# A decoder layer on one core: gate and up projections as a 2x2 block product with seven products, the down projection as its own stage

## The chip, the cores and the metric

The kernel runs on one core of one Trainium2 chip. The metric is device time in microseconds of one execution, the median of several runs; less is better. TensorE (PE in the profile; PEld is its weight loads) multiplies, VectorE (DVE) and ScalarE (ACT) do element-wise work, GpSimd (POOL) issues some stores, and SyncE (SP) issues the loads, in program order.

## The reference

One hybrid decoder layer for 512 tokens of width 2048, in float32. Two attentions side by side, a memory cross-attention and a SwiGLU feed-forward follow each other, each with a scaled residual and a layer norm. The change concerns the last part (D_MODEL is 2048, D_FF is 5632):

```python
c = memory_cross_attention(h, mem, w_q_mem[l], w_kv_mem[l], w_o_mem[l])
h = layer_norm(ALPHA * h + c, ln2_g[l], ln2_b[l])
gate, up = jnp.split(h @ w_gate_up[l], 2, axis=-1)      # [512, 2048] @ [2048, 11264]
f = (jax.nn.silu(gate) * up) @ w_down[l]                # [512, 5632] @ [5632, 2048]
h = layer_norm(ALPHA * h + f, ln3_g[l], ln3_b[l])
```

## The kernel before

**Number format.** Products run in float32r. Every operand is split into hi (rounded to float32r) and lo = x - hi. `split` (L102 to 104) is one ScalarE cast that writes hi and one VectorE subtraction that writes lo. A product is three matmuls (`mm3`, L124 to 129): hi by hi, hi by lo, lo by hi.

**Weights.** A weight unit is 128 x 1024 numbers, 512 KB. SP loads it into a staging tile (`ws`, L112), then it is split. There are three buffers each of staging, hi and lo. `next_unit` keeps two units ahead of the one in use. The tile `wgu` is a unit of gate or up weights, `wdn` one of down weights.

**Order.** TensorE's and SP's instructions run in the order of the program text. VectorE's and ScalarE's are ordered by a scheduler as the kernel is built. `Side` places side work (layer norms, transposes) between the weight units.

**The feed-forward.** There are 44 hidden tiles f of 128 features. Gate and up of one f are each 2 units, 16 contraction blocks of 128, so 48 matmuls of 512 tokens each into one PSUM bank (`gate_up`, tile `gu`). `glu` makes silu(gate) times up and splits it into `fh` and `fl`, which stay in SBUF. The hidden tiles go in pairs, in chunks of 6, 6, 5, 3 and 2 pairs; behind the pairs of a chunk its down products run (`down`, tiles `dn_*`), 4 column blocks of 512, added into the residual `y`. So gate/up and down alternate.

**The first four hidden tiles.** While the second 256 tokens still go through layer norm 2, `swiglu_halves` runs the first 2 pairs for tokens 0 to 255 alone (tile `gh`, 256 columns), and then, with the same weights loaded again, for tokens 256 to 511. That is 768 matmuls of 256 columns; the other 40 hidden tiles are 3840 of 512 columns. `put` transposes the normed rows (`h2tr`) and splits them into `h2h` and `h2l`, the moving operands.

**The tail.** The down weights of the last 2 pairs are kept in SBUF (`resident`), so that the last products run by token block and layer norm 3 can begin early.

Of the kernel before, what the change touches and what calls it, by code (L numbers as in the profile page):

```python
# [1018 lines left out]
```

## Time and profile before

| | |
|---|---|
| runs | 2735.85, 2737.0, 2740.66 us; median 2737.0 us |
| span of the profiled execution | 2737.2 us |
| TensorE busy | 2709.0 us (99%) |
| VectorE, ScalarE busy | 1303.8 us (48%), 942.6 us (34%) |
| moved by DMA | 325.57 MB, 119 GB/s over the span |

The result gives no time of its own for the profiled execution beside its span; 0.2 us lie between the span and the median of the runs. A matmul's duration in the profile contains the filling and draining of the array, which overlap with its neighbours; how fast matmuls follow each other is read from their start times.

### The profile page before, as it was taken

Reading aid. Unit: us, or ns where it says so; the run is one execution under the profiler, and the core shown is the slowest. Engines: PE = TensorE matmul, PEld = TensorE weight load, DVE = VectorE, ACT = ScalarE, POOL = GpSimd, SP = SyncE. Lnnn points to the kernel's source line nnn. Section 1 sums busy time; section 2 is a strip of 40 time slices with the busy share of each in tenths; the row PEclk is TensorE's granted clock in tenths of the full one; section 3 lists DMA queues with packets and bytes.
Section 4 is the critical chain, followed back from the end, with each engine's and each line's share of the span. In section 5 each row is a group of like instructions: output and inputs, shape, how many; then the busy total and the mean of one; then the engine's idle time right before and its main releaser. Section 6 shows DMA issues by size and latency. Waiting matters only on the chain.

```text
span 2737.2 us, 33827 instructions
## 1 busy us (share of the span) xinstructions
PE 2709.0 (99%) x14024; PEld 2301.8 (84%) x14024; DVE 1303.8 (48%) x1659; ACT 942.6 (34%) x1338; POOL 67.7 (2%) x109
## 2 busy tenths in 40 slices
PE   9999999999999999999999999999999999999998
PEld 7877777899988889988988888888888888888886
DVE  4258888986523753459632223222232223323247
ACT  3246556664421453345522212222222222222230
POOL 0001110100000000000000000000000000000001
PEclk9999999999999999999999999999999999999999
DMA  5322222346732662345543233322323232332341
GB/s 180 103 79 69 74 74 77 109 154 198 249 123 97 234 239 93 108 149 175 182 142 99 94 100 93 100 95 98 99 94 100 94 100 96 96 100 93 100 138 62
DMA packets 91146, 325.57 MB, mean 119 GB/s; under 512 B 10480, under 2 KB 10736, under 8 KB 90992
## 3 DMA queue, kind: packets, MB, share of 16 engines
q1 hardware_dynamic: 87408, 310.83, 34.9%
q0 software_dynamic: 3584, 12.58, 1.2%
q8 instruction: 110, 1.80, 0.3%
q14 instruction: 44, 0.36, 0.0%
HBM read 306.59 MB, written 16.78 MB: 118 GB/s over the span
## 4 chain that ended last, share of the span: by engine, by line
PE 95%; DVE 2%; ACT 2%; issue 0%; POOL 0%; DMA 0%; DVEq 0%; SPq 0%; POOLq 0%
PE gu L127 11%; PE gu L129 11%; PE gu L128 11%; PE mvp L127 1%; PE pjkb L127 1%; PE mvp L129 1%; PE mkp L129 1%; PE mkp L128 1%; PE mkp L127 1%; PE gh L127 1%; PE gh L128 1%; PE kq L129 1%; PE gh L129 1%; PE kq L128 1%; PE mvp L128 1%; PE kq L127 1%
## 5 line engine op out<-in xcount | busy, mean ns | idle before, releaser
L104 DVE TENSOR_TENSOR wgu_1l<-wgu_1s,wgu_1h 128x1024 fp32r<-128x1024 f32 x96 | 117.6, 1225 | 324.6 <-ACT wgu_1h L103 324.6
L127 PE MATMUL gu<-h2h,wgu_0h 128*128 128x512 f32 x640 | 249.0, 389 | 0.0
L128 PE MATMUL gu<-h2l,wgu_0h 128*128 128x512 f32 x640 | 249.0, 389 | 0.0
L129 PE MATMUL gu<-h2h,wgu_0l 128*128 128x512 f32 x640 | 249.0, 389 | 0.0
L127 PE MATMUL gu<-h2h,wgu_1h 128*128 128x512 f32 x640 | 249.0, 389 | 0.0
L128 PE MATMUL gu<-h2l,wgu_1h 128*128 128x512 f32 x640 | 249.0, 389 | 0.0
L129 PE MATMUL gu<-h2h,wgu_1l 128*128 128x512 f32 x640 | 249.0, 389 | 0.0
L103 ACT CAST wgu_0h<-wgu_0s 128x1024 fp32r<-128x1024 f32 x96 | 101.0, 1053 | 370.7 <-PE gu L128 315.8
L103 ACT CAST wgu_1h<-wgu_1s 128x1024 fp32r<-128x1024 f32 x96 | 101.1, 1053 | 325.8 <-PE gu L128 152.9
L104 DVE TENSOR_TENSOR wgu_0l<-wgu_0s,wgu_0h 128x1024 fp32r<-128x1024 f32 x96 | 117.5, 1224 | 184.7 <-ACT wgu_0h L103 184.7
L129 PEld LDWEIGHTS gu<-h2h,wgu_0l 128*128 128x128 f32 x640 | 120.3, 188 | 25.0
L127 PEld LDWEIGHTS gu<-h2h,wgu_1h 128*128 128x128 f32 x640 | 120.3, 188 | 25.0
L128 PEld LDWEIGHTS gu<-h2l,wgu_0h 128*128 128x128 f32 x640 | 120.1, 188 | 25.1
L128 PEld LDWEIGHTS gu<-h2l,wgu_1h 128*128 128x128 f32 x640 | 120.2, 188 | 24.8
L129 PEld LDWEIGHTS gu<-h2h,wgu_1l 128*128 128x128 f32 x640 | 120.0, 188 | 24.9
L127 PEld LDWEIGHTS gu<-h2h,wgu_0h 128*128 128x128 f32 x640 | 120.0, 188 | 24.7
L848 DVE TENSOR_TENSOR sg<-sg,gu 128x512 f32<-128x512 f32 x40 | 27.5, 687 | 134.2 <-PE gu L129 134.2
L104 DVE TENSOR_TENSOR wdn_0l<-wdn_0s,wdn_0h 128x1024 fp32r<-128x1024 f32 x20 | 24.5, 1225 | 66.9 <-ACT wdn_0h L103 66.9
L104 DVE TENSOR_TENSOR wdn_2l<-wdn_2s,wdn_2h 128x1024 fp32r<-128x1024 f32 x20 | 24.5, 1225 | 66.1 <-ACT wdn_2h L103 66.1
L104 DVE TENSOR_TENSOR wdn_1l<-wdn_1s,wdn_1h 128x1024 fp32r<-128x1024 f32 x20 | 24.5, 1223 | 65.2 <-ACT wdn_1h L103 65.2
L104 DVE TENSOR_TENSOR wdn_3l<-wdn_3s,wdn_3h 128x1024 fp32r<-128x1024 f32 x20 | 24.5, 1224 | 63.3 <-ACT wdn_3h L103 63.3
L332 DVE TENSOR_TENSOR_SCAN a<-ones,nl 128x128 f32<-128x128 f32 (+3 forms) x64 | 49.8, 811 | 10.1 <-POOL nl L329 9.9
(1923 smaller groups left out, 7052.3 us busy)
## 6 DMA issues: line engine op xcount, KB each, us to landing
wgu_0s<-in_w_gu SPq DMA_DIRECT2D x96, 512.0 KB, 3.5
wgu_1s<-in_w_gu SPq DMA_DIRECT2D x96, 512.0 KB, 3.4
wdn_0s<-in_w_dn SPq DMA_DIRECT2D x22, 512.0 KB, 3.5
wdn_1s<-in_w_dn SPq DMA_DIRECT2D x22, 512.0 KB, 3.4
wdn_2s<-in_w_dn SPq DMA_DIRECT2D x22, 512.0 KB, 3.5
wdn_3s<-in_w_dn SPq DMA_DIRECT2D x22, 512.0 KB, 3.4
wmv_0s<-in_w_mv SPq DMA_DIRECT2D x16, 512.0 KB, 3.6
wmv_1s<-in_w_mv SPq DMA_DIRECT2D x16, 512.0 KB, 3.6
```

Of the source, the lines that this page charges most:

```text
L103: nc.scalar.copy(hi, src)
L104: return nc.vector.tensor_tensor(lo, src, f32(hi), op=ALU.subtract)
L127: nc.tensor.matmul(acc, lh, rh, start=first, stop=False)
L128: nc.tensor.matmul(acc, lh, rl, start=False, stop=False)
L129: nc.tensor.matmul(acc, ll, rh, start=False, stop=last)
L332: nc.vector.tensor_tensor_scan(a[:, h, :nk][:, ::-1], ones.to_broadcast([P, nk]), nlt[:, h, :nk][:, ::-1], 0.0, op0=ALU.mult, op1=ALU.add)
L848: nc.vector.tensor_tensor(sg, sg, ua, op=ALU.mult)
```

## The change

**The block product.** The 512 tokens by 2048 inputs are taken as 2x2 blocks: a11 (tokens 0 to 255, inputs 0 to 1023), a12, a21, a22. For each hidden tile the weights are 2x2 blocks too: input half by gate or up, 1024 x 128 each. The product of these, eight block products before, is made of seven, with sums on both sides:

- on the token side once: s1 = a21 - a22, s3 = a11 - a21, s2 = s1 - a11 and s4 = a12 + s2, each split into hi and lo, beside a11, a12 and a22;
- on the weight side for every hidden tile, by VectorE: three additions on a loaded piece `xw` (1024, 512 and 512 columns for four loaded blocks of 512), then the splits `wh` and `wl` of seven blocks, 1792 columns for each quarter of the contraction;
- on the result: the seven products lie in four PSUM banks (tile `zz`, two buffers), and `finish` adds them up in the tile `e`.

All matmuls of this stage have 256 moving columns. The weights come as pieces of 1 MB (`w_st`), two for each hidden tile, each into its own buffer (`x0`, `x1` of the pool `pq`, one each; `xw0` and `xw1` below). Three buffers of `wh` and `wl` hold the quarters.

**The early part.** In place of `swiglu_halves`, a11 and a12 times the gate weights of 12 hidden tiles (`EARLY`, tile `ge`, 576 matmuls of 256 columns) run while the second half of the tokens is normed. Their two results go to memory (`early_d`) and come back for `finish`; for these 12 tiles five products are left and five blocks (1280 columns) to split. The side work now also makes the sums and splits on the token side (`second_half`).

**Memory.** silu(gate) times up goes to memory (`f_d`, 1 MB for a pair), and so does `y` (`y_d`). The pools of SBUF and PSUM are closed and opened anew for the gate/up stage and once more for the down stage. That stage has chunks of 8, 6, 6 and 2 pairs and loads `fx`, `fh`, `fl` and `yf` through SP, between the weights. Its matmuls and its tail are as before.

The core of the diff:

```diff
-FF_CHUNKS = [6, 6, 5, 3, 2]
+FF_CHUNKS = [8, 6, 6, 2]
+EARLY = 12
...
+    for f in range(EARLY):
+        acc = ps_lin(f"ge{f}")
         for u in range(2):
             w = next_unit()
             for c in range(8):
-                mm3(a, at(w, ALL, cs(c, P)), at(hc(8 * u + c), ALL, cols), u == 0 and c == 0, u == 1 and c == 7)
+                mm3(acc[:, cs(u, 256)], at(w, ALL, cs(c, P)), a_block(("a11", "a12")[u], c), c == 0, c == 7)
             side.run(SIDE3)
+        e = otile(f"ee{f}")
+        urgent(nc.scalar.copy, e[:, 256:512], acc[:, 0:256])
+        urgent(nc.vector.tensor_tensor, e[:, 0:256], e[:, 256:512], acc[:, 256:512], op=ALU.add)
+        nc.gpsimd.dma_start(early_d[f], e)
+    side.drain()
+    (pq, ps) = open_pools(1, [("pq", 1), ("ps", 1)])
+    PRODUCTS = [("a11", 1, 2, 0), ("a12", 2, 0, 0), ("s4", 3, 1, 1), ("s1", 4, 3, 0), ("s3", 5, 2, 1),
+                ("s2", 6, 0, 1), ("a22", 7, 1, 0)]
...
+        for f, h in pieces:
+            x = pq.tile([P, 8, 512], F32, tag=f"x{h}", name=f"xw{h}")
+            lowest = 3 if f < EARLY else 1
+            nc.sync.dma_start(x[:, 0:4], io["w_st"][f, h].rearrange("p (b n) -> p b n", b=4))
+            nc.vector.tensor_tensor(x[:, 4:6], x[:, 1:4:2], x[:, 0:1].to_broadcast([P, 2, 512]), op=ALU.add)
+            nc.vector.tensor_tensor(x[:, 6], x[:, 4], x[:, 3], op=ALU.add)
+            nc.vector.tensor_tensor(x[:, 7], x[:, 6], x[:, 2], op=ALU.add)
+            for k in range(2):
+                hi = pq.tile([P, 7, 256], F32R, tag=f"wh{n % 3}", name=f"wh{n % 3}")
+                lo = pq.tile([P, 7, 256], F32R, tag=f"wl{n % 3}", name=f"wl{n % 3}")
+                src = x[:, lowest:8, cs(k, 256)]
+                split(hi[:, lowest - 1:7], lo[:, lowest - 1:7], src)
...
+    def finish(f, z, e):
+        e1 = e[:, 7]
+        tt = nc.vector.tensor_tensor
+        if f < EARLY:
+            urgent(tt, e[:, 2], e1, z[:, 0, 256:512], op=ALU.add)
+        else:
+            urgent(nc.scalar.copy, e1, z[:, 2, 0:256])
+            urgent(tt, e[:, 0:3:2], z[:, 0].rearrange("p (b n) -> p b n", b=2),
+                   e[:, 7:8].to_broadcast([P, 2, 256]), op=ALU.add)
+        urgent(tt, e[:, 1], e[:, 2], z[:, 2, 256:512], op=ALU.add)
+        urgent(tt, e[:, 5:7], z[:, 3:4, 0:256].to_broadcast([P, 2, 256]), e[:, 1:3], op=ALU.subtract)
+        urgent(tt, e[:, 3:5], e[:, 1:7:5], z[:, 1].rearrange("p (b n) -> p b n", b=2), op=ALU.add)
+        sg, fh, fl = otile(f"sg{f}"), otile(f"fh{f}", F32R), otile(f"fl{f}", F32R)
+        s2 = sg.rearrange("p (b n) -> p b n", b=2)
+        nc.scalar.activation(s2, e[:, 0:4:3], AF.Silu)
+        tt(s2, s2, e[:, 4:6], op=ALU.mult)
+        split(fh, fl, sg)
+        nc.gpsimd.dma_start(f_d[f // 2, 0][:, cs(f % 2, 512)], f32(fh))
+        nc.gpsimd.dma_start(f_d[f // 2, 1][:, cs(f % 2, 512)], f32(fl))
+    for f in range(NFT):
+        z = ps.tile([P, 4, 512], F32, tag="zz", name=f"zz{f}", bufs=2)
+        for step in range(4):
+            hi, lo = next_weights()
...
+                    for i, (l, r) in enumerate(((wh, ah), (wh, al), (wl, ah))):
+                        nc.tensor.matmul(out_, l, r, start=begin and i == 0 and bank not in seen,
+                                         stop=step == 3 and k == 1 and i == 2, skip_group_check=True)
...
+        finish(f, z, e)
+    pt, pw, pg, ps = open_pools(2, [("pt", 2), ("pw", 3), ("pg", 4), ("ps", 1)])
...
+                if first and nb == 0:
+                    if i + 2 < len(prs):
+                        fs[prs[i + 2]] = f_in_x(prs[i + 2])
+                    if i % 2 == 0:
+                        nc.sync.dma_start(y[i // 2][0], y_d[i // 2, 0])
+                if first and nb == 1 and i < len(chunks[1]):
+                    fs[chunks[1][i]] = f_in_m(chunks[1][i])
```

**VectorE inside the gate/up stage.** Before, in the middle of the stage: one hidden tile has four unit splits, one product `sg` and one split `fl`.

```order
L104 TENSOR_TENSOR wgu20_1_1l_15340<-wgu20_1_1s_15337,wgu20_1_1h_15339 128x1024
L104 TENSOR_TENSOR wgu21_0_0l_15371<-wgu21_0_0s_15368,wgu21_0_0h_15370 128x1024
L104 TENSOR_TENSOR wgu21_0_1l_15401<-wgu21_0_1s_15398,wgu21_0_1h_15400 128x1024
L848 TENSOR_TENSOR sg10_0_15428<-sg10_0_15428,gu20_1_15367 128x512
L104 TENSOR_TENSOR wgu21_1_0l_15437<-wgu21_1_0s_15434,wgu21_1_0h_15436 128x1024
L104 TENSOR_TENSOR fl10_15305<-sg10_0_15428,fh10_15304 128x512
```

Now, behind the twelfth hidden tile, part of the cycle of one hidden tile (`wl0` to `wl2` are the three weight buffers, `xw0` and `xw1` the two pieces):

```order
L983 TENSOR_TENSOR sg16_15304<-sg16_15304,e_15210 128x512
L116 TENSOR_TENSOR wl0_15417<-xw0_15411,wh0_15416 128x1792
L116 TENSOR_TENSOR fl16_15306<-sg16_15304,fh16_15305 128x512
L946 TENSOR_TENSOR xw1_15524<-xw1_15524 128x1024
L947 TENSOR_TENSOR xw1_15524<-xw1_15524 128x512
L948 TENSOR_TENSOR xw1_15524<-xw1_15524 128x512
L116 TENSOR_TENSOR wl1_15464<-xw0_15411,wh1_15463 128x1792
L116 TENSOR_TENSOR wl2_15530<-xw1_15524,wh2_15529 128x1792
L120 TENSOR_TENSOR e_15420<-zz17_15313,e_15420 128x2x256
L946 TENSOR_TENSOR xw0_15621<-xw0_15621 128x1024
L120 TENSOR_TENSOR e_15420<-e_15420,zz17_15313 128x256
L947 TENSOR_TENSOR xw0_15621<-xw0_15621 128x512
```

`wl1_15464` is the last reader of piece `xw0_15411`; the next piece in that buffer, `xw0_15621`, is loaded behind it and stands two VectorE instructions further on.

**VectorE where the 256-column products of the first half end.** Before:

```order
L104 TENSOR_TENSOR wgu1_3_0_1l_12341<-wgu1_3_0_1s_12338,wgu1_3_0_1h_12340 128x1024
L848 TENSOR_TENSOR sg1_0_1_12368<-sg1_0_1_12368,gh2_1_1_12307 128x256
L104 TENSOR_TENSOR wgu1_3_1_0l_12377<-wgu1_3_1_0s_12374,wgu1_3_1_0h_12376 128x1024
L104 TENSOR_TENSOR fl1_11391<-sg1_0_1_12368,fh1_11390 128x256
L104 TENSOR_TENSOR wgu1_3_1_1l_12407<-wgu1_3_1_1s_12404,wgu1_3_1_1h_12406 128x1024
```

Now, from the last early unit on (`hr01`, `s2`, `s4` belong to the token side):

```order
L116 TENSOR_TENSOR wge11_1l_12197<-wge11_1s_12194,wge11_1h_12196 128x1024
L854 TENSOR_TENSOR hr01_11294<-hr01_11294,hr00_11209 128x1024 x2
L116 TENSOR_TENSOR s2l_12257<-hr00_11209,s2h0_12255 128x1024
L116 TENSOR_TENSOR s2l_12257<-hr00_11209,s2h1_12256 128x1024
L120 TENSOR_TENSOR ee11_12292<-ee11_12292,ge11_12230 128x256
L116 TENSOR_TENSOR s4l_12287<-hr01_11294,s4h_12286 128x1024 x2
L946 TENSOR_TENSOR xw0_12307<-xw0_12307 128x1024
L947 TENSOR_TENSOR xw0_12307<-xw0_12307 128x512
L948 TENSOR_TENSOR xw0_12307<-xw0_12307 128x512
L946 TENSOR_TENSOR xw1_12320<-xw1_12320 128x1024
L116 TENSOR_TENSOR wl0_12313<-xw0_12307,wh0_12312 128x1280
```

Between the split of the last early unit and the first `wl` stand eleven VectorE instructions, where before the next unit's split followed.

**SP where the gate/up stage ends.** Before, at the first change from gate/up to down weights:

```order
L112 DMA wgu11_1_0s_13406<-in_w_gu 128x1024
L112 DMA wgu11_1_1s_13436<-in_w_gu 128x1024
L112 DMA wdn0_0s_13467<-in_w_dn 128x1024
L112 DMA wdn1_0s_13497<-in_w_dn 128x1024
L112 DMA wdn2_0s_13534<-in_w_dn 128x1024
```

Now:

```order
L945 DMA xw1_20774<-in_w_st 128x2048
L1021 DMA fx0_20992<-f_d_10634 128x1024 x2
L1021 DMA fx1_20995<-f_d_10634 128x1024 x2
L124 DMA wdn0_0s_21000<-in_w_dn 128x1024
L124 DMA wdn1_0s_21006<-in_w_dn 128x1024
L124 DMA wdn2_0s_21012<-in_w_dn 128x1024
L1021 DMA fx2_21018<-f_d_10634 128x1024 x2
L1044 DMA yf0_0_20984<-y_d_10632 128x1024
L124 DMA wdn3_0s_21046<-in_w_dn 128x1024
L1021 DMA fx3_21052<-f_d_10634 128x1024 x2
```

The first down weights now stand behind 2 MB of hidden tiles, and further megabytes stand between the weights that follow.

## Rows read from the trace of the kernel before

**Rows 1.** Page: span; busy us (share) and instructions of TensorE, VectorE, ScalarE.

```profile
span 2737.2 us, 33827 instructions
...
PE 2709.0 (99%) x14024; PEld 2301.8 (84%) x14024; DVE 1303.8 (48%) x1659; ACT 942.6 (34%) x1338; POOL 67.7 (2%) x109
```

**Rows 2.** Page: the chain of work that ended last, shares by engine.

```profile
PE 95%; DVE 2%; ACT 2%; issue 0%; POOL 0%; DMA 0%; DVEq 0%; SPq 0%; POOLq 0%
```

**Rows 3.** Waits of PE: engine, line, releaser: us in total, times, longest.

```profile
PE trb L351 <- ACT a L335: 9.4, 5, 1.9
PE zb L136 <- DVE qb L108: 0.3, 1, 0.3
```

**Rows 4.** By tile: matmuls, duration in ns min/median/max, first and last start us.

```profile
L127 PE MATMUL gu<-h2h,wgu_0h x640: 389/389/396, 1375.5 to 2609.7; 128*128 128x512 f32 x160
...
L127 PE MATMUL dn_0a<-wdn_0h,fh x80: 389/389/389, 1549.6 to 2630.8; 128*128 128x512 f32 x80
...
L127 PE MATMUL mkp<-mh,wmk_0h x128: 283/283/283, 645.7 to 734.6; 128*128 128x256 f32 x128
...
L129 PE MATMUL mkp<-mh,wmk_1l x128: 283/283/283, 648.8 to 737.8; 128*128 128x256 f32 x128
```

**Rows 5.** Busy us (instructions) by stretch: PE, PEld, DVE, ACT, POOL; clock, DMA share, GB/s.

```profile
1279.00:1327.00 48.00, 48.00 (x402) 47.84 (x401) 41.02 (x63) 31.90 (x42) 0.00 (x0) 1.00 0.57 176
1327.00:1375.50 48.50, 48.50 (x407) 48.50 (x406) 23.85 (x25) 19.75 (x25) 0.00 (x0) 1.00 0.66 207
1375.50:1549.60 174.10, 174.10 (x770) 144.19 (x770) 49.07 (x48) 41.76 (x49) 0.00 (x0) 1.00 0.32 106
```

**Rows 6.** Groups of VectorE by form: busy us, mean ns of one | idle before, releaser.

```profile
L104 DVE TENSOR_TENSOR wgu_1l<-wgu_1s,wgu_1h 128x1024 fp32r<-128x1024 f32 x96 | 117.6, 1225 | 324.6 <-ACT wgu_1h L103 324.6
...
L104 DVE TENSOR_TENSOR fl<-sg,fh 128x512 fp32r<-128x512 f32 x40 | 27.4, 684 | 0.0
...
L104 DVE TENSOR_TENSOR fl<-sg,fh 128x256 fp32r<-128x256 f32 x8 | 3.3, 416 | 0.5 <-ACT fh L103 0.5
```

**Rows 7.** Timeline of VectorE: start us, us, instruction [idle before].

```profile
1309.59 1.22 DVE L104 TENSOR_TENSOR wgu_1l<-wgu_1s,wgu_1h 128x1024 fp32r<-128x1024 f32 x1
1310.72 0.75 DVE L667 SCALAR_TENSOR_TENSOR y<-y,n2mv,ln_b 128x512 f32<-128x512 f32 x1
1311.38 1.22 DVE L104 TENSOR_TENSOR wgu_0l<-wgu_0s,wgu_0h 128x1024 fp32r<-128x1024 f32 x1
1312.52 1.28 DVE L104 TENSOR_TENSOR h2l<-h2tr,h2h 128x512 fp32r<-128x512 f32 x2
```

**Rows 8.** Groups of ScalarE by form.

```profile
L103 ACT CAST wgu_1h<-wgu_1s 128x1024 fp32r<-128x1024 f32 x96 | 101.1, 1053 | 325.8 <-PE gu L128 152.9 <-issue 148.6 <-PE dn_3d L129 13.2
...
L103 ACT CAST fh<-sg 128x512 fp32r<-128x512 f32 x40 | 24.5, 613 | 0.0
...
L847 ACT ACTIVATE sg<-gu 128x512 f32<-128x512 f32 x40 | 23.5, 588 | 0.0
```

**Rows 9.** DMA issues: queue, count, KB each, median us to landing.

```profile
wgu_0s<-in_w_gu SPq DMA_DIRECT2D x96, 512.0 KB, 3.5
...
wmk_1s<-in_w_mk SPq DMA_DIRECT2D x16, 512.0 KB, 4.3
...
out<-y SPq DMA_DIRECT2D x16, 256.0 KB, 2.4
```

**Rows 10.** DMA view of 640 to 740 us: GB/s in 40 slices of 2.5 us.

```profile
GB/s 111 193 203 7 198 246 244 328 144 216 357 246 239 203 208 43 279 313 216 259 238 203 267 238 61 224 326 172 221 292 239 221 228 180 128 262 244 221 236 262
```

**Rows 11.** Chain over 0 to 15 us, TensorE's first matmuls: start, us, what.

```profile
8.34 0.43 PE v0b L128
...
13.28 0.23 PE v0b L129
```

**Rows 12.** Timeline, down projection: a split ends, its buffer's next load is issued.

```profile
2002.36 1.23 DVE L104 TENSOR_TENSOR wdn_2l<-wdn_2s,wdn_2h 128x1024 fp32r<-128x1024 f32 x1 [4.22 <-ACT wdn_2h L103]
...
2003.62 0.33 SPq L112 DMA_DIRECT2D wdn_2s<-in_w_dn  x1
```

More of the change, by code (lines that the diff above doesn't have):

```diff
@@ L40 @@
 AHEAD = 2
-HALVED = 2
 TURN = 2
@@ L811, in layer, with put @@
     gb2 = load_gb("ln2_g", "ln2_b")
-    put, hc = transposed("h2")
+    y_d = dram.tile([NT, 2, P, 1024], F32, name="y_d")
+    early_d = dram.tile([EARLY, P, 512], F32, name="early_d")
+    f_d = dram.tile([NFT // 2, 2, P, 1024], F32, name="f_d")
+    raw = {}
+    blocks = {}
+    def put(t, nb, bank):
+        key = (t // 2, nb // 2)
+        if key not in raw:
+            raw[key] = xtile(1, [P, 8, 256], f"hr{key[0]}{key[1]}", F32)
+        tr = bank(f"h2tr{t}_{nb}")
+        for c in range(4):
+            o = (nb % 2) * 512 + c * P
+            nc.tensor.transpose(tr[:, cs(c, P)], y[t][nb // 2][:, o:o + P], ident)
+        c0 = (nb % 2) * 4
+        urgent(nc.scalar.copy, raw[key][:, c0:c0 + 4, cs(t % 2, P)], tr.rearrange("p (c n) -> p c n", c=4))
+        yield
@@ new lines, in block, with x_halves, of, m_halves @@
+    def block(name, tile_of):
+        hi, lo = tile_of(name + "h"), tile_of(name + "l")
+        blocks[name] = hi, lo
+        return hi, lo
+    def x_halves(half):
+        def of(name):
+            w = xtile(half, [P, 8, 256], name)
+            return [w[:, 0:4], w[:, 4:8]]
+        return of
+    def m_halves(name):
+        return [mtile([P, 4, 256], f"{name}{j}") for j in range(2)]
+    def split_block(name, src, hi, lo):
+        for j in range(2):
+            split(hi[j], lo[j], src[:, cs(j, 4)])
+            yield
@@ L813, in layer, with a_block, keep @@
+    def a_block(name, c):
+        hi, lo = blocks[name]
+        return hi[c // 4][:, c % 4], lo[c // 4][:, c % 4]
+    def keep(t):
+        for i in range(2):
+            nc.gpsimd.dma_start(y_d[t, i], y[t][i])
+        yield
     for half in range(2):
@@ new lines, in layer, with weights @@
+    pieces = [(f, h) for f in range(NFT) for h in range(2)]
+    ready = []
+    def weights():
+        n = 0
+        for f, h in pieces:
[10 more added lines that the diff above has]
+                split(hi[:, lowest - 1:7], lo[:, lowest - 1:7], src)
+                n += 1
+                yield hi, lo
@@ new lines, in layer, with y_tile, f_load, f_in_x @@
+    pt, pw, pg, ps = open_pools(2, [("pt", 2), ("pw", 3), ("pg", 4), ("ps", 1)])
+    def y_tile(t, i):
+        return mtile([P, 1024], f"yf{t}_{i}", F32) if t == 1 else ttile(t, [P, 1024], f"yf{t}_{i}")
+    y[:] = [[y_tile(t, i) for i in range(2)] for t in range(NT)]
+    def f_load(pr, tiles):
+        for part, ft in enumerate(tiles):
+            nc.sync.dma_start(f32(ft), f_d[pr, part].rearrange("p (c n) -> p c n", c=2))
+        return tiles
+    def f_in_x(pr):
+        ft = xtile(pr % 2, [P, 2, 2, 512], f"fx{pr}")
+        return f_load(pr, [ft[:, part] for part in range(2)])
@@ L889, in down, with f_in_m @@
+    def f_in_m(pr):
+        return f_load(pr, [mtile([P, 2, 512], f"fh{pr}"), mtile([P, 2, 512], f"fl{pr}")])
+    fs, res = {}, {}
+    def down(prs, blocks, first=False, ahead_of=None):
         for nb in blocks:
@@ L924, in resident @@
                     yield
-    down(chunks[-2], f1, [0])
+    source = down_units()
+    c0, c1, c2, c3 = chunks
+    for pr in c0[:2]:
+        fs[pr] = f_in_x(pr)
+    down(c0, range(4), first=True)
+    gb = load_gb("ln3_g", "ln3_b")
+    down(c1, range(4), ahead_of=c2)
+    fs[c2[-1]] = f_in_m(c2[-1])
+    tc.keep_in_program_order(nc.scalar.preload_act_table_set("natural_log_exp_and_others"))
+    down(c2, [0])
     side.add(resident())
-    down(chunks[-2], f1, [1, 2, 3])
+    down(c2, [1, 2, 3], ahead_of=c3)
     side.drain()
```

166 lines of the change are left out of this document (85 added, 81 removed).

## The prediction

> **What bounds the kernel now.** I read the page first: TensorE is busy for 99% of the span [rows 1], and the chain of work that ended last is 95% TensorE [rows 2]. The view of waits confirms it: the longest sum of TensorE's waits on one releaser is 9.4 us, all in the attention [rows 3]. In the feed-forward it never waits. VectorE is busy for less than half of the span, but in the stretch that the early part takes the place of it is busy for 41.0 of 48 us [rows 5], so the mean hides where it is short. What the change can win is therefore how fast matmuls follow each other; what it can lose is the cover that the other engines and the loads now give TensorE without a gap.
>
> **Matmul rates.** Durations overlap, so I take starts. The 8 hidden tiles from 1375.5 us to the first down product at 1549.6 us are 768 matmuls of 512 columns: 0.2267 us each. The `mkp` stage is 768 matmuls of 256 columns from 645.7 to 737.8 us: 0.1201 us each [rows 4]. Two short ones cost 6% more than a long one.
>
> **Products.** Before, gate/up is 3840 x 0.2267 + 768 x 0.1201 = 870.5 + 92.2 = 962.7 us. Now it is 12 x 48 early, 12 x 120 and 32 x 168, together 7392 matmuls of 256 columns: 887.8 us. The change takes away 74.9 us, not an eighth of 962.7 (120), since all columns now run at the dearer rate. The down products (2112 matmuls of 512) are equal.
>
> **Prices on VectorE and ScalarE.** A VectorE operation of 1024, 512, 256 columns takes 1225, 684, 416 ns [rows 6], but the next independent one starts about 0.085 us before its end (1309.59 to 1310.72 us) [rows 7]: 1.14, 0.60, 0.33 us in a row. No row has 1280 or 1792 columns; on the same line they are 1.41 and 1.95 us. ScalarE's cast takes 1053 and 613 ns for 1024 and 512 [rows 8], so 1.27 and 1.71 us. A waiting engine starts some 0.03 us behind its releaser [rows 12].
>
> **A 1 MB load.** The trace has none, and much hangs on it; call its time to landing L. 512 KB land in 3.5 us, 256 KB (stores) in 2.4 us [rows 9]. On that slope L is 3.5 + 2 x 1.1 = 5.7 us at most for an idle queue. At the fastest rate of any slice, 357 GB/s [rows 10], 512 KB more take 1.5 us, so L = 5.0 us at least. I take 5.2 us, nearer the lower end: some of the 1.1 us is the difference between a load and a store.
>
> **Hidden tiles 0 to 11.** TensorE needs 120 x 0.1201 = 14.4 us for each. VectorE has four splits (5.6), six additions on weights (4.7) and `finish` (3.1): 13.4 us. That would fit, but it waits: the additions on `xw0` must end before ScalarE casts (1.27 us) and VectorE subtracts, and the next load of `xw0` starts only behind the second of these splits. From the first addition on a piece to that split there are in VectorE's order 1.14 + 0.60 + 1.41 + 0.60 + 1.41 + 1.29 us, 1.3 us of waiting for the cast, and 1.41 + 1.50: with hand-overs 10.8 us. Then L. The cycle is 10.8 + 5.2 = 16.0 us, so TensorE loses 12 x 1.6 = **19 us**. If the load lands in time, the 13.4 us, the wait for the cast and 0.5 us of dependent starts remain: 15.2 us a tile (+9); with L = 5.7 us it is +25.
>
> **Hidden tiles 12 to 43.** TensorE needs 168 x 0.1201 = 20.2 us. VectorE has four splits (7.8), six additions (4.7), `finish` (3.3): 15.8 us. The same loop through `xw0` is 13.4 us of VectorE, 1.2 us of waiting for ScalarE (silu, then a cast of 1.71 us before the split may run) and hand-overs: 14.8 + L = 20.0 us. It fits, with 0.2 us to spare. I charge **2 us** for the catching up at tile 12, not more, since the split quarters lie about 6 us ahead of TensorE. Each further microsecond of L costs 32 us here.
>
> **The early part.** 576 x 0.1201 us and the transposes are some 72.7 us. VectorE's work there is 22 unit splits, 10 token-side splits and 8 sums at 1.14, the norm and residual (some 19 us) and the evictions (4): 68.7 us. Before it had 41.0 us of work in the first 48 [rows 5]. I charge **2 us** of gaps (0 to 6).
>
> **First change of pools.** From the last early unit's split to the first `wl` stand 6 x 1.14 + 0.33 + 2.5 + 1.14 + 1.41 = 12.2 us on VectorE, where before another unit's split followed at once. A unit lasts 2.9 us on TensorE, and a split can be one or two units ahead: TensorE stands for 12.2 - 2.9 - (0 to 5.8) = 3.5 to 9.3 us. I take **7 us**, since VectorE is too full to be far ahead. Queued behind this are all products of tile 0.
>
> **Second change of pools.** The `fx0` load waits for a11, whose last product ends about 4.3 us before the stage does; `fx1` and `wdn0` queue behind it. These 2.5 MB at 345 GB/s (just below the fastest slice) and 2 us of latency end 9.3 us later, 5 us behind the stage's end, then come cast and subtraction (2.3 us): **8 us**, between 5 (fx0 alone late) and 14 (at 250 GB/s).
>
> **The clock.** The profile's granted clock is 1.00 in all rows shown [rows 5], the level of 2.4 GHz, yet TensorE's first matmuls after the start, where it had done nothing, begin 0.43 us apart, later 0.23 [rows 11]. Up to 12.6 us this costs some 3 us. Whether a gap of 7 us brings that back no row tells: 0 to 3 us at each change, I take 2 each, **4 us**.
>
> **The first down passes.** Per weight unit (5.44 us) SP now loads 0.5 MB of weights, 1 MB of hidden tiles and 0.25 MB of `y`: 337 GB/s against a mean of 218 and a fastest slice of 357 in the busiest stretch [rows 10]. Two units of prefetch cover it at 340, hence 0; at 250 GB/s the eight units' 13.5 MB take 54 us instead of 43.5, and the second pass is alike: up to 15 us.
>
> **Sum.** 2737.2 - 74.9 + 19 + 2 + 2 + 7 + 8 + 4 = 2704.3 us. The span is 0.2 us above the median of the runs, so 2704 us stands for the runs too. Of 74.9 us won, 42 are given back.
>
> **The rivals.** *A: everything is covered.* Loads land early, VectorE's 15.2 us cycle alone limits tiles 0 to 11 (+9), the changes cost 3.5 and 5, the clock stays: 2737.2 - 74.9 + 9 + 3.5 + 5 = 2680 us. For it: 0.2 us of slack in the long tiles. Against: VectorE is full exactly where the stages meet.
>
> *B: the reloads starve the down stage.* As the forecast with 15 us more: 2719 us. For it: 512 KB landed in 4.3 instead of 3.5 us in a stretch of about 220 GB/s [rows 9, 10]. Against: the demand lasts for only two passes.
>
> *C, the slower side: the piece buffers.* Each of `xw0` and `xw1` has one buffer, so L stands in a loop with VectorE. With 512 KB in 4.3 us [rows 9] and 2.2 us for the other half, L = 6.5 us: 12 x (17.3 - 14.4) = 35 and 32 x (21.3 - 20.2) = 35 us, so 2704 - 19 + 35 + 35 = 2755 us. It decides from L = 6.1 us on: there 12 x 2.5 + 32 x 0.7 = 52 us, together with the 23 us of the other terms, use up the 74.9. For it: 0.5 MB stores of the hidden tile and a 256 KB load share the queues. Against: these come earlier in the cycle than the load of `xw0`.
>
> The Trainium skill bears on C ("DMA: Bandwidth & Descriptors", Bandwidth, Measured): its table, for loads issued from GpSimd, has 6.15 us for 1 MB, by which C would hold at its turning point, with about 2740 us. The same page's fit (Anatomy of one DMA: 2.0 us and bytes over 436 GB/s) gives 4.4 us for 1 MB, by which A or the forecast would. For 512 KB the fit gives 3.2 us where the rows have 3.5; no run so far shows 1 MB.
>
> *D: the change doesn't do what it says.* The order of the program has 7392 products of 256 columns, so the eighth is really gone; only the rate of 0.1201 could fail. `mkp` held it over 92 us with a weight load for every matmul. I give this no share.
>
> **How the numbers follow.** Forecast (2690 to 2722 us) 0.50; A 0.10; B 0.12; C 0.28, of which 0.08 lies near the turning point. A measurement of this kernel can tell about 0.2%, 5.5 us, from no change. Faster 0.72, same 0.08, slower 0.20. The range 2682 to 2752 us leaves out the lower part of A and the upper of C.
>
> **What would show it.** Right: `zz` matmuls 0.120 us apart; 16 us for each of tiles 0 to 11 and 20.2 us for the later ones; `xw` loads landing in about 5.2 us; two gaps of 7 and 8 us of TensorE at the changes of pools. Wrong: later tiles above 20.5 us with VectorE idle until an `xw` load lands (C); gaps of TensorE among the first sixteen down units (B); tiles 0 to 11 at 14.4 us (A); 256-column starts further apart than 0.12 us without any wait.

## The result and the profile after

The changed kernel takes 2713.7 us, the median of four runs (2712.2 to 2715.1), against 2738.8 us for the kernel before on the same chip: a ratio of 0.9912, with a 95% interval of 0.9898 to 0.9926. It is faster by 0.9%, 25 us where the prediction said 33. The profiled execution's span is 2710.2 us, 27.0 us less than before's 2737.2 [rows 1].

From the page: the span, busy us and share by engine, and the chain that ended last.

```profile
span 2710.2 us, 40347 instructions
...
PE 2646.9 (98%) x16808; PEld 2360.3 (87%) x16808; DVE 1735.7 (64%) x2101; ACT 1059.2 (39%) x1390; POOL 125.5 (5%) x217
...
PE 80%; DVE 9%; DMA 4%; ACT 4%; issue 3%; POOL 0%; DVEq 0%; SPq 0%; ACTq 0%; POOLq 0%
```

TensorE's share of the chain went from 95 to 80% [rows 2]: the other engines now stand on the path. Where, the view of TensorE's waits shows (engine, line, releaser: us in total, times, longest):

```profile
PE zz L1006 <- DVE wl L116: 17.2, 14, 2.5
PE trb L363 <- ACT a L347: 9.6, 5, 1.9
PE zz L1006 <- ACT wh L115: 8.2, 1, 8.2
PE dn_0a L139 <- ACT wdn_0h L115: 7.0, 1, 7.0
```

The second row is the 9.4 us of before [rows 3]. The other three are new. The same by stretch: early part, first change of pools, tiles 0 to 11, tiles 12 to 43, second change, the first down pass, the rest of the down products (from, to, us, then busy us and instructions of PE, PEld, DVE, ACT and POOL, granted clock, DMA share, GB/s):

```profile
1282.70:1355.50 72.80, 71.76 (x609) 71.33 (x607) 63.66 (x85) 39.44 (x54) 8.10 (x15) 1.00 0.65 228
1355.50:1363.90 8.40, 0.23 (x3) 0.03 (x1) 8.14 (x10) 2.66 (x4) 0.54 (x1) 0.72 0.44 157
1363.90:1558.50 194.60, 178.78 (x1440) 176.07 (x1441) 163.56 (x187) 74.36 (x72) 11.86 (x22) 0.95 0.49 176
1558.50:2195.00 636.50, 634.93 (x5378) 633.12 (x5376) 515.19 (x508) 255.81 (x221) 34.56 (x64) 1.00 0.36 131
2195.00:2202.00 7.00, 0.03 (x1) 0.00 (x0) 3.87 (x6) 2.66 (x4) 1.08 (x2) 0.78 1.00 377
2202.00:2250.00 48.00, 47.49 (x190) 37.81 (x191) 12.26 (x10) 9.43 (x9) 0.00 (x0) 0.93 0.92 356
2250.00:2654.00 404.00, 404.00 (x1733) 325.52 (x1732) 125.06 (x125) 82.31 (x79) 0.00 (x0) 1.00 0.39 138
```

**Where the 27 us come from.** Early part, gate/up and both changes of pools take 919.3 us (1282.7 to 2202.0), where the 768 short and 3840 long gate/up products of before take 95.6 + 870.5 = 966.1: 46.8 us won. The down products take 451.8 us, where before's 1920 at 0.2267 us are 435.3: **16.5 us lost, 12.7 of them with no wait and at full clock**. All that comes ahead of the feed-forward ends 2.9 us later, though up to the memory output (`pvo`) no line of it was changed. These 12.7 and 2.9 us were not foreseen, and runs 1 to 4 show that they are one effect. (Run n is the run of experiment n below.)

**Matmul rates changed in code that did not.** A stretch of 100 us inside the down products (before: gate/up and down products, which ran equally fast), of before and of after:

```profile
2300.00:2400.00 100.00, 100.00 (x442) 82.81 (x442) 32.80 (x35) 20.05 (x19) 0.00 (x0) 1.00 0.30 96
```

```profile
2300.00:2400.00 100.00, 100.00 (x430) 80.55 (x430) 27.21 (x26) 18.87 (x18) 0.00 (x0) 1.00 0.33 113
```

The clock is 1.00, TensorE never waits, and it gets 430 matmuls done instead of 442. By starts (waits and the lower clock left out), `dn` went from 0.2267 to 0.2333 us. `wo`, `vo` and `v`, far ahead of the change, rose too, to 0.2317 to 0.2333; `dl`, whose weights lie in the pool of the activations (`px`), stayed at 0.2267. Of the 256-column products, `mkp` went the other way, from 0.1200 to 0.1178 us, and `zz` runs at 0.1178 in nearly all of tiles 12 to 43, not at the 0.1201 that the sum used.

### The profile page after: what moved, and what is told of

The parts are those of the page before. It is cut to its first block, busy times and chain, and to the rows that moved or that the text cites. A ratio compares the mean times of both kernels' runs of the same rounds, so it can differ in the third digit from the quotient of the medians.

```text
span 2710.2 us, 40347 instructions
## 1 busy us (share of the span) xinstructions
PE 2646.9 (98%) x16808; PEld 2360.3 (87%) x16808; DVE 1735.7 (64%) x2101; ACT 1059.2 (39%) x1390; POOL 125.5 (5%) x217
## 4 chain that ended last, share of the span: by engine, by line
PE 80%; DVE 9%; DMA 4%; ACT 4%; issue 3%; POOL 0%; DVEq 0%; SPq 0%; ACTq 0%; POOLq 0%
PE zz L1006 23%; DMA xw<-in_w_st 3%; DVE wl L116 1%; PE kq L140 1%; PE mvp L139 1%; DVE a L344 1%; PE mvp L141 1%; PE vo L141 1%; PE vo L140 1%; PE kq L141 1%; PE vo L139 1%; PE kq L139 1%; PE mvp L140 1%; PE pjqa L139 1%; PE pjqa L140 1%
## 5 line engine op out<-in xcount | busy, mean ns | idle before, releaser
L115 ACT CAST wh<-xw 128x1792 fp32r<-128x1792 f32 (+1 forms) x176 | 276.8, 1579 | 303.9 <-DVE xw L948 172.2
L116 DVE TENSOR_TENSOR wl<-xw,wh 128x1792 fp32r<-128x1792 f32 (+1 forms) x176 | 328.6, 1876 | 73.9 <-ACT wh L115 72.0
L946 DVE TENSOR_TENSOR xw<-xw 128x1024 f32<-128x1024 f32 x88 | 107.6, 1222 | 62.6 <-DMA xw<-in_w_st 62.3
L1006 PE MATMUL zz<-s4h,wl 128*128 128x256 f32 x352 | 100.2, 285 | 15.7 <-DVE wl L116 15.7
L1006 PE MATMUL zz<-s1l,wh 128*128 128x256 f32 x352 | 99.6, 283 | 0.0
L1006 PE MATMUL zz<-s3l,wh 128*128 128x256 f32 x352 | 99.6, 283 | 0.0
L1006 PE MATMUL zz<-s1h,wl 128*128 128x256 f32 x352 | 99.5, 283 | 0.0
L1006 PE MATMUL zz<-s3h,wh 128*128 128x256 f32 x352 | 99.5, 283 | 0.0
L1006 PE MATMUL zz<-s1h,wh 128*128 128x256 f32 x352 | 99.3, 282 | 0.0
L1006 PE MATMUL zz<-s3h,wl 128*128 128x256 f32 x352 | 99.3, 282 | 0.0
```

Source lines behind the costliest of these rows:

```text
L115: nc.scalar.copy(hi, src)
L116: return nc.vector.tensor_tensor(lo, src, f32(hi), op=ALU.subtract)
L946: nc.vector.tensor_tensor(x[:, 4:6], x[:, 1:4:2], x[:, 0:1].to_broadcast([P, 2, 512]), op=ALU.add)
L1006: nc.tensor.matmul(out_, l, r, start=begin and i == 0 and bank not in seen, stop=step == 3 and k == 1 and i == 2, skip_group_check=True)
```

## The experiments

The theory of the first two: the change opens the pool `sm` earlier, which moves all weights in SBUF. Before, every large tile started at the same place modulo 4096; now the weights (`pw`, `pq`) lie 704 bytes, 192 modulo 256, behind the activations (`px`, `pm`), and the place of a matmul's two operands to each other sets its rate.

**1. The kernel before, with one pool moved.**

```diff
 pm = ctx.enter_context(tc.tile_pool(name="pm", bufs=14))
+sm = ctx.enter_context(tc.tile_pool(name="sm", bufs=2))
...
-sm = ctx.enter_context(tc.tile_pool(name="sm", bufs=2))
```

> The kernel before, with nothing changed but the place of one pool: sm is opened between pm and pt, as in the changed kernel, so that the tiles of pt, pg and pw (weights among them) lie 8896 bytes later in each SBUF partition, at 480 instead of 288 modulo 512, while the activations (px, pm) stay at 288. Theory (the place of a matmul's two operands to each other sets how fast matmuls follow each other): products with weights as the 512-column moving operand go from 0.2267 to 0.233 us (3840 matmuls, +25.7 us), mkp and mvp from 0.1200 to 0.1178 us (1536, -3.4), gh likewise (768, -1.7), gu between -6 us and nothing: 2753 to 2759 us. Rival (the rates changed in the changed kernel for another reason: its stages, its clock, its DMA load): no change, 2738 us, all rates as before.

Measured: 2773.7 us, 36 us slower (ratio 1.0135, 1.012 to 1.015). One moved line costs more than the whole change brings. `dn`, `v` and `vo` show 0.2333 us, `wo` 0.2317, `mkp` 0.1175. It is more than expected because `gu`, for which I had at best no loss, went to 0.2313: 3840 x 0.0046 = 17.7 us. The terms by their rates add up to some 34 us. The rival is dead: no stage, clock or load of the changed kernel is in this one. Its row, beside the two above:

```profile
2300.00:2400.00 100.00, 100.00 (x431) 80.38 (x430) 30.89 (x32) 19.88 (x20) 0.00 (x0) 1.00 0.30 95
```

**2. The changed kernel, with the operands in line again.**

```diff
+tiny = ctx.enter_context(tc.tile_pool(name="tiny", bufs=2))
 px = ctx.enter_context(tc.tile_pool(name="px", bufs=4))
...
-mx = sm.tile([P, 4], F32, tag="mx", name=f"mx{j}_{st}")
+mx = tiny.tile([P, 4], F32, tag="mx", name=f"mx{j}_{st}")
```

(and so for `nm`, `rs`, `bst` and `mv`)

> The changed kernel, with the 704 bytes of small tiles of sm (mx, nm, rs, bst, mv) in a pool of their own ahead of px: all large tiles then lie at the same residue modulo 512 (480), as they did before (288). Theory that only the place to each other counts: wo, vo, pvo and dn back at 0.2267 us (-25.7 us), mkp, mvp back at 0.1200 (+3.4), ge and the zz of the 32 long tiles at 0.1200 (+1.3 and +12.4): 2705 us; 2692 if zz stays at 0.1178 us. Rival (the residue itself counts, not the difference): all rates as in the changed kernel, 2714 us.

Measured: 2703.2 us, 10.4 less than the changed kernel. `dn` is back at 0.2267 us and `mkp` at 0.1200, and `zz` at 0.1200: tiles 12 to 43 take 20.18 us each instead of 19.88. So the difference of the two places counts, since all tiles stand 704 bytes further on than before the change, and the rates are those of before. The starts of the feed-forward fit too: 1277.4 to 1278.5 us in the runs with this layout (2, 3, 9, 11 and 12; 1281.2 in run 10) and 1285.1 to 1285.7 in the four others with the changed kernel's layout (5 to 8), against 1279.9 before. So the loss ahead of the feed-forward is rather 5 to 8 us, and the changed kernel's profiled execution, with 2.9, shows the least of it.

```profile
1700.00:1800.00 100.00, 100.00 (x836) 100.00 (x835) 80.44 (x80) 40.49 (x34) 5.40 (x10) 1.00 0.36 129
2300.00:2400.00 100.00, 100.00 (x443) 82.84 (x442) 27.57 (x27) 18.91 (x18) 0.00 (x0) 1.00 0.35 118
```

In the first row (tiles 12 to 43) the changed kernel has 852 matmuls, in the second (down products) 430.

**3. Each width at its better place.** As the last one, and in the gate/up stage alone 176 unused numbers, 704 bytes, ahead of the weights:

```diff
-(pq, ps) = open_pools(1, [("pq", 1), ("ps", 1)])
+(gap, pq, ps) = open_pools(1, [("gap", 1), ("pq", 1), ("ps", 1)])
+nc.vector.memset(gap.tile([P, 176], F32, name="gap"), 0.0)
```

> The changed kernel with the small tiles in a pool ahead of px (all large tiles at one residue modulo 512) and, in the gate/up stage alone, 704 unused bytes ahead of the weight pool, which put the stationary weights 192 modulo 512 behind the activations again. Theory (the place of the two operands to each other counts, and long and short matmuls want opposite places): dn, wo, vo, v and pvo at 0.2267 us as in the run with the small tiles first (2703 us), zz at 0.118 us as in the changed kernel: tiles 12 to 43 at 19.9 instead of 20.2 us, -10 us: 2693 us. Rival (the faster 256-column rate has another cause, the wl and wh places among themselves for instance): 2703 us.

Measured: 2693.4 us, as the theory had it; 19.92 us for each of tiles 12 to 43 and 0.2267 us for `dn`.

**4. The effect by itself.**

> No layer at all: TensorE alone runs 34 groups of 48 matmuls (float32r, weights changed for every matmul as in the kernel, in the order hi hi, hi lo, lo hi). In each group the stationary operand lies at a fixed place and the moving one 0, 32, 64, ... bytes further on modulo 4096; groups pa to po have 512 columns with differences of 0, 32, 64, 96, 128, 160, 192, 224, 256, 288, 320, 384, 448, 512 and 1024 bytes, pp and pq both operands 288 bytes further with differences of 0 and 192; pr to pz and then za to zh the same with 256 columns. Its time is not the layer's. Theory (the difference of the two places modulo 512 sets the rate): 512 columns 0.2267 us at differences of 0, 512 and 1024 and 0.233 at 192; 256 columns 0.1200 and 0.1178; pp like pa, pq like pg. Rival (not the operands' places to each other but what ScalarE and VectorE write meanwhile): every group of one width at one rate.

No other engine works while these groups run, and the rates still differ, so the rival falls. Of the trace's tile view: matmuls, duration in ns (min/median/max), first and last start in us; differences of 0, 192 and 256 bytes with 512 columns, 0 and 192 with 256 columns, and 192 again with both operands 288 bytes further on:

```profile
L76 PE MATMUL pa<-big x48: 389/389/389, 34.1 to 44.8; 128*128 128x512 f32 x48
L76 PE MATMUL pg<-big x48: 391/393/398, 100.9 to 111.8; 128*128 128x512 f32 x48
L76 PE MATMUL pi<-big x48: 389/389/395, 123.3 to 133.9; 128*128 128x512 f32 x48
L76 PE MATMUL pr<-big x48: 278/283/283, 222.6 to 228.2; 128*128 128x256 f32 x48
L76 PE MATMUL px<-big x48: 278/281/283, 256.8 to 262.3; 128*128 128x256 f32 x48
L76 PE MATMUL pzh<-big x48: 276/276/286, 313.6 to 319.0; 128*128 128x256 f32 x48
```

Mean distance of the starts, in ns, by the place of the moving operand less that of the stationary one (288 bytes give the rates of 32):

| difference, bytes | 0 | 32 | 64 | 96 | 128 | 160 | 192 | 224 | 256 | 320 | 384 | 448 | 512 | 1024 |
|---|---|---|---|---|---|---|---|---|---|---|---|---|---|---|
| 512 columns | 226.7 | 233.4 | 229.1 | 233.6 | 233.4 | 234.1 | 233.2 | 233.2 | 226.8 | 229.1 | 232.2 | 233.3 | 227.6 | 226.7 |
| 256 columns | 119.7 | 117.9 | 117.9 | 119.8 | 118.6 | 118.7 | 117.8 | 118.3 | 119.9 | 117.9 | 118.7 | 114.0 | 119.6 | 120.0 |

The period is 256 bytes (0, 256, 512 and 1024 agree, and 64 with 320), not the 512 that I had expected; only the short ones at 192 and 448 differ. Of the differences tried, long matmuls are fastest at 0 modulo 256, by 1 to 3%; short ones are at or near their slowest there. At 192 and 448, the same modulo 256, short ones have two rates, 117.8 and about 114 ns. With both operands moved by 288 bytes and a difference of 192, long ones have 233.3 (`pq`), short ones 113.7 (`pzh`).

In the kernels the sign matters: the weights that lie 704 bytes behind are the moving operand in `dn` (192 in this table, 233.2 for a measured 233.3), and the stationary one in `zz`, `mkp` and `gu` (64 in this table, 117.9 for the 117.8 of `zz`). `wo`, at 231.7, mixes 192 with 0: six of its eight lo operands lie in a pool that moved along with the weights. For `gu` in run 1 the table has 229.1 and the run 231.3, so the difference alone doesn't give every rate.

The next four ask what holds tiles 0 to 11 at 16.2 us, where TensorE needs 14.1.

**5. Smaller pieces.**

```diff
-x = pq.tile([P, 8, 512], F32, tag=f"x{h}", name=f"xw{h}")
-nc.sync.dma_start(x[:, 0:4], io["w_st"][f, h].rearrange("p (b n) -> p b n", b=4))
+for k in range(2):
+    x = pq.tile([P, 8, 256], F32, tag=f"x{h}{k}", name=f"xw{h}{k}")
+    nc.sync.dma_start(x[:, 0:4], io["w_st"][f, h, k].rearrange("p (b n) -> p b n", b=4))
```

> The changed kernel, with four piece buffers of 512 KB for two of 1 MB: each quarter of the contraction is loaded, added up and split on its own, and its buffer comes free after one split instead of two. Twelve additions of 512, 256, 256 columns a tile for six of 1024, 512, 512: +0.4 us of VectorE. Theory (tiles 0 to 11 are held by the loop through the single piece buffer, 10.8 us and a 4.8 us load): the loop is now some 8 us for a quarter with four buffers, and a tile goes from 16.2 to between 14.2 (TensorE) and 15.2 us (VectorE and its waits); tiles 12 to 43 stay at 19.9 us; 2714 - 12 to 24 = 2690 to 2702 us. Rival (VectorE's own work limits these tiles): no gain, or a loss of 12 x 0.4 = 5 us: 2714 to 2719 us.

Measured: 2709.0 us; tiles 0 to 11 at 15.95 us. The 3 us won in these tiles are not fewer waits: by starts, TensorE loses 19.5 us to waits there in the changed kernel and 20.8 here, but 8.1 and 1.9 us to the lower clock. So neither theory nor rival: the buffers were not what held these tiles, or something took their place. SP's own waits in these tiles (queue, line, releaser), first in the changed kernel, then here, show a candidate:

```profile
SPq L995 <- DVE sg L983: 74.1, 11, 8.9
SPq L945 <- DVE wl L116: 72.6, 17, 10.7
```

```profile
SPq L995 <- DVE xw L948: 76.9, 8, 10.8
SPq L946 <- DVE wl L116: 45.5, 22, 8.8
SPq L995 <- DVE xw L949: 25.9, 2, 14.6
```

L995 is the load of `e`. It waits for VectorE to be done with the one `e` buffer, and the pieces of the next tile stand behind it on SP, in the changed kernel too.

**6. That load off SP's queue.** As the last one, and:

```diff
-nc.sync.dma_start(e[:, 0:8:7], early_d[f].rearrange("p (b n) -> p b n", b=2))
+nc.gpsimd.dma_start(e[:, 0:8:7], early_d[f].rearrange("p (b n) -> p b n", b=2))
```

> The quarter pieces of 512 KB (four buffers) as in the run before, and the load of the early results into e issued by GpSimd instead of SP. In the run with quarter pieces alone, tiles 0 to 11 took 15.95 us: SP stood at the load of e until VectorE's sg (the last reader of the one e buffer) had ended, up to 14.6 us, and the four weight pieces of the next tile were issued behind it. Theory (these tiles are held by a loop of SP's queue: sg, e's load, weight pieces, additions, splits, finish): off SP's queue, the pieces are issued as their buffers come free, and a tile takes 14.2 to 14.8 us (TensorE's 120 x 0.118 = 14.1; VectorE's 13.5 us busy): 12 x 1.3 = -16 us against 2709, so 2690 to 2695 us. Rival (VectorE's order and its waits for ScalarE's casts hold them): no change, 2709 us.

Measured: 2698.6 us, from 2675.0 to 2705.7; the profiled execution was the slowest, with 15.49 us a tile. SP now waits for buffers alone, and by starts TensorE's waits in these tiles fall from 20.8 to 14.9 us, so SP's queue was part of it; yet the tiles don't reach 14.8 us. VectorE is busy for 141.6 of the 160 us from 1390 to 1550 and waits another 16.6 us for pieces, at the places that its order, fixed when the kernel is built, gives them. That leaves VectorE's work and the waits that its order puts into it as the limit. This is argued from its full time: no run took work off VectorE in these tiles.

**7. Every piece loaded twice.**

```diff
 nc.sync.dma_start(x[:, 0:4], io["w_st"][f, h].rearrange("p (b n) -> p b n", b=4))
+nc.sync.dma_start(x[:, 0:4], io["w_st"][f, h].rearrange("p (b n) -> p b n", b=4))
```

> The changed kernel, with each 1 MB weight piece loaded twice in a row into its buffer, so that the time L to landing goes from 4.8 to about 9.6 us (7 us if the two overlap). Theory (L stands in a loop with VectorE: 10.8 + L for tiles 0 to 11, 14.8 + L for the later ones): 20.4 us and 24.4 us a tile for 16.2 and 19.9, so +50 and +144 us, about 2908 us (2777 at L = 7). Rival (the loads are hidden behind TensorE and VectorE): below 2730 us.

Measured: 2755.9 us (one execution), 42 more, not 194. The second load is issued when the first has landed, so from the first issue to the first addition L is 11.6 us (SP and VectorE, timelines; the piece issued at 1443.45):

```profile
1443.45 0.33 SPq L945 DMA_DIRECT2D xw<-in_w_st  x1
1449.55 0.33 SPq L946 DMA_DIRECT2D xw<-in_w_st  x1
```

```profile
1455.05 1.23 DVE L947 TENSOR_TENSOR xw<-xw 128x1024 f32<-128x1024 f32 x1 [2.42 <-DMA xw<-in_w_st]
```

Tiles 0 to 11 take 18.9 us and the later ones 20.2. That L stands in a loop fits, since both got slower and VectorE waits for the loads; that the rest of the loop is 10.8 or 14.8 us does not. Here 18.9 - 11.6 = 7.3 us remain: with the second load the built order sets both splits of a piece close behind its additions. What the old order would cost at this L was not measured.

**8. The second change of pools.** The down weights first:

```diff
-pt, pw, pg, ps = open_pools(2, [("pt", 2), ("pw", 3), ("pg", 4), ("ps", 1)])
+pw, pt, pg, ps = open_pools(2, [("pw", 3), ("pt", 2), ("pg", 4), ("ps", 1)])
...
+ahead += [unit(*next(source)) for _ in range(2)]
 for pr in c0[:2]:
     fs[pr] = f_in_x(pr)
```

> The changed kernel with the first two down weight units loaded ahead of the hidden tiles fx0 and fx1 at the second change of pools, and the pool of the down weights opened first, so that its staging buffers lie where the weight pieces were. Theory (TensorE stands 7.3 us there because wdn0 is queued behind 2 MB of hidden tiles that wait for a11): the cast of wdn0 needs its buffer free of the last but one quarter (5 us before the stage's end), and fx0 alone lands some 3 us behind the end of the stage: the gap falls from 7.3 to 2 to 4 us, 2709 to 2711 us. Rival (the gap is made by the hidden tiles, f_d's last stores, or the casts behind finish on ScalarE): the gap stays at 7 us, 2714 us.

Measured: the gap falls from 7.3 to 5.0 us, so part of it was the queue; the time, 2712.8 us (2709.2 to 2715.1), can't be told from the changed kernel's. ScalarE's timeline names what is late next: the first cast stands behind `sg`, the last tile's silu, which waits for `finish` on VectorE.

```profile
2199.07 0.63 ACT L982 ACTIVATE sg<-e 128x512 f32<-128x512 f32 x1 [2.65 <-DVE e L120]
2199.61 1.03 ACT L115 CAST wdn_0h<-wdn_0s 128x1024 fp32r<-128x1024 f32 x1
```

**9 and 10. Together, and the first change of pools.** Runs 3, 6 and 8 in one kernel (the two early down weights of run 8 also put at high priority in the built order), then the same with three steps of side work behind each early unit instead of two (`SIDE3`).

> The changed kernel with the edits of four runs together: small tiles first and 704 unused bytes ahead of the gate/up weights (2693 us alone), quarter pieces with e's load on GpSimd (tiles 0 to 11 at 15.2 to 15.8 us a tile instead of 16.2, -7 us), down weights ahead of the hidden tiles (gap of 5 instead of 7.3 us, -2 us). If the effects are independent: 2684 us, with 0.2267 us for the 512-column products, 0.118 for zz. Rival (TensorE's waits only move: what tiles 0 to 11 gain is lost again behind them, and the pads take their gain from each other): 2693 us.

> As the run before it, with three steps of side work behind each early unit instead of two, which puts VectorE's token-side splits s2 and s4 ahead of the last early units; in the built order only the sums of the last early tile then stand between its products and the additions on the first weight piece. Theory (the first change of pools costs 8.4 us because VectorE has 5.9 us of s2 and s4 splits and a sum to do first): the gap falls to 5 to 6 us, 2681 us, unless TensorE waits as long inside the early part. Rival (the load of the first weight piece is what comes last): the gap stays at 8 us, 2684 us.

Measured: 2678.1 us (2655.4 to 2683.9), a ratio to before of 0.9754 (0.9724 to 0.9783). The effects add up: the profiled execution took 2683.9 us where the sum was 2684. This is the fastest version, 36 us ahead of the changed kernel. With the side work pulled forward the first gap falls from 8.0 to 4.0 us, so VectorE's splits of `s2` and `s4` did make half of it. But the early part grows from 73.6 to 83.0 us, and the median is 6 us slower, 2684.1 us (2680.5 to 2688.0). The two profiled executions differ by 1.3 us alone, since tiles 0 to 11 take 15.05 us each here and 15.53 without this edit. TensorE's waits in that run:

```profile
PE ge L142 <- DVE wge_1l L117: 5.0, 3, 1.7
...
PE zz L1008 <- ACT wh L116: 3.7, 1, 3.7
...
PE ge L142 <- DVE wge_0l L117: 2.1, 2, 1.4
```

The wait moved into the early part, where VectorE is nearly full up to 1352 us. The last two early units wait for their loads as well: SP issues these only when VectorE's earlier splits have freed the staging buffers, and ScalarE's casts stand for them (0.7 us, and here 2.7):

```profile
1357.82 1.05 ACT L116 CAST wge_1h<-wge_1s 128x1024 fp32r<-128x1024 f32 x1 [2.66 <-DMA wge_1s<-in_w_ge]
```

**11 and 12. Why executions of that kernel differ by 28 us.**

> The kernel with the four edits together once more, for another profiled execution: six executions of it lay between 2655.4 and 2683.9 us, and the profiled one (2683.9) had zz at 0.1178 us in nearly all tiles. In the changed kernel and in the run with the down weights first, some tiles in a row had zz 0.1133 us apart, from one wait of TensorE to the next. Theory (the 256-column rate with operands 192 bytes apart has two values, and which one holds is settled anew at each wait): an execution near 2656 us has zz at 0.1133 us in most of tiles 12 to 43, 5376 x 0.0045 = 24 us, one near 2680 us at 0.1178. Rival (something else differs between executions, loads or waits): both have zz at 0.1178 us and differ in gaps.

> As the run before it, a third profiled execution of the same kernel: near 2656 us with zz at 0.1133 us in most tiles, or near 2680 us with zz at 0.1178 us (theory); rival: the same rate whatever the time.

Measured: 2683.5 and 2681.7 us (one execution each), with `zz` at 0.1178 us in tiles 13 to 43 of both. Neither came near 2656 us, so the theory was not put to its test, and the cause stays open. That two rates exist for the same operands is shown, though, in the run with the down weights first. Two stretches of its tiles 12 to 43:

```profile
1558.00:1700.00 142.00, 141.48 (x1243) 141.15 (x1243) 121.31 (x119) 60.66 (x52) 7.55 (x14) 1.00 0.37 134
1715.00:1850.00 135.00, 134.51 (x1141) 134.05 (x1140) 110.37 (x110) 52.44 (x47) 6.59 (x13) 1.00 0.36 128
```

One matmul in 0.1142 us, then in 0.1183, at the same clock; between them lies a wait of TensorE of 0.9 us. By starts, waits left out, it is 0.1133 us in each of tiles 13 to 18 and 0.1178 in tiles 20 to 25.

## Why the prediction was right, and where it was not

The sign and the range held, and the time lies in the forecast's own range. But several terms are off, and their errors partly cancel: the down products and what lies ahead of the feed-forward took 17 us more than the sum has, tiles 12 to 43 took 11 less. That the sum came within 6 us of the span is partly luck.

**Products: the rates were taken as fixed.** "The down products (2112 matmuls of 512) are equal" and 0.1201 us for 256 columns both rest on rates read where both operands lay in line. The change moved them. The 7392 short products gained some 20 us on the 887.8 (0.1173 us on average, as some stretches of `zz` run at 0.1133); the down products lost 12.7 (1920 x 0.0066). By their rates `v`, `wo`, `vo` and `pvo` lost 11 us and `mkp`, `mvp` and `kq` won 5; the profiled executions show 2.9 us net ahead of the feed-forward, the later runs 5 to 8 (run 2). Case D, "only the rate of 0.1201 could fail", looked at one width, and only for the worse. This was the step that failed. The change's edit of the pools stands in the diff; what it does to addresses I had not asked. Without that effect on the long products the changed kernel takes 2693 us (run 3).

**Tiles 0 to 11: the size was right, partly by luck, the reason half.** 16.2 us against 16.0, but 0.7 of the 16.2 us are the lower clock (8.1 us by starts), for which the prediction had 2 us after the change of pools and nothing in the tiles. The load lands in 4.8 us (5.2 estimated):

```profile
xw<-in_w_st SPq DMA_DIRECT2D x88, 1024.0 KB, 4.8
```

The page of the Trainium skill that the prediction weighed ("DMA: Bandwidth & Descriptors") has a fit (Anatomy of one DMA) that gives an estimate of 4.4 us and a table (Bandwidth, Measured, for loads issued from GpSimd) that has 6.15. The trace's 4.8 us lies nearer the fit. But the loop through the piece buffer alone was not what held these tiles. With more and smaller buffers they fall only to 15.95 (the clock, run 5), and with SP's queue freed as well to between 15.05 and 15.5 us (runs 6 and 9 to 12). That is near the other bound of that step, the 15.2 us for a load that lands in time. VectorE is busy 13.6 us of each tile and waits 1.6 for the casts and 0.6 for loads (views of its waits in this stretch: 19.1 and 6.6 us). Of the 25 us that TensorE loses here beyond its 14.1 a tile, some 8 are the clock, 2 of them right behind the change of pools.

**Tiles 12 to 43.** 19.9 us: TensorE's own 168 x 0.1178 = 19.8 and little more, as "It fits" said. Of VectorE's 55.7 us of waits for loads hardly anything reaches TensorE, which waits twice here, 1.5 us in all.

**Early part and changes of pools.** 1.0 us of gaps for 2, 8.4 for 7, 7.3 for 8. The reasons were right too: VectorE's chain of `s2`, `s4` and additions (run 10, for half of the gap), and SP's order (run 8, for 2.3 us of it; what then comes is ScalarE's order). The prediction's own terms for the second change, 5 and 2.3 us, add up to 7.3, the measured value; the 8 in its sum is rounded up.

**The clock.** 4 us charged, 5 measured at the two changes: after the first, the matmuls start 0.213 us apart until 1369.4, about 2 us lost; after the second 0.427 us apart until 2209.0, 3.1 us lost. What was missed: it also falls four times inside tiles 0 to 11 (granted 0.95 in that stretch), some 6 us more.

**The first down passes.** Charged nothing; 190 matmuls in the first 48 us at 356 GB/s. Of the 3.7 us that they take beyond 0.2333 us each, 3.1 are the clock. So B is refuted, though the time lies near its 2719: the lost time is in the rate, not in gaps.

**The rivals.** C would have needed L = 6.1 us; with L at 11.6 us the loss was 42 us and not the 32 us for each microsecond that it reckoned for the long tiles alone, since with the second load the built order is another one (run 7). A failed: the changes of pools cost 8.4 and 7.3 us and not 3.5 and 5, tiles 0 to 11 took 16.2 and not 15.2, and the clock fell.

## What to carry to other kernels

Before costing an edit that opens, closes or reorders pools, compare the SBUF addresses of the operands before and after: here 704 bytes of small tiles moved most matmul rates by 1 to 3%, and placing them anew and padding one stage brought another 20 us where the whole change had brought 25. When a chain of waits looks like a loop through one buffer, list also the engine's fixed order and what stands ahead on the load queue: here smaller buffers alone took nothing off TensorE's waits, and the freed queue did. Split time lost to waits from time lost to the clock before crediting an edit. A wait moved forward on an engine that is already full there came back as several small ones (run 10).
